# A retention loop with the output norm's channel gain moved into the output weight, and its loads in another order

## The chip, the cores and the metric

The kernel runs on one core of a Trainium2 chip. A core has a matrix engine (TensorE, PE in the profile; its weight loads are listed apart as PEld), a vector engine (DVE), a scalar engine (ACT), a general engine (POOL) and a sync engine (SP), which here issues most of the DMAs. Each engine works through its own queue in order; engines wait for one another by semaphores. The metric is the time of one execution on the device in microseconds.

## The reference

One inference step of a small decoder trunk with two layers: a retention layer and a sliding-window attention layer (called swa in the code), for a prompt of 1024 positions with 1024 channels and for 8 single new tokens, all in fp32. What bears on the change is the retention layer of the prompt:

```python
def retention_layer(x, S0, g_norm, w_in, g_out, w_out):
    h = rmsnorm(x, g_norm)
    proj = h @ w_in
    q, k, v, gate = jnp.split(proj, [RET_QK, 2 * RET_QK, 2 * RET_QK + RET_V], axis=-1)
    ...                       # 4 heads, 256 wide in q and k, 512 wide in v
    o, S = retention_scan(q, k, v, S0)      # 8 chunks of 128 positions
    o = rmsnorm(o, g_out.reshape(RET_HEADS, RET_DV)).reshape(B, L, RET_V)
    o = o * jax.nn.silu(gate)
    return x + o @ w_out, S.astype(S0.dtype)
```

`rmsnorm(o, g_out)` divides each row of a head's 512 channels by its root mean square and multiplies each channel by its gain. The gate is multiplied in after that, and then the 2048 channels are contracted with `w_out`. A gain per channel of `o` is therefore also a gain per row of `w_out`. The scan returns the final state of each head, 256 x 512, which is an output of its own.

## The kernel before, in words

fp32 matmuls are done as three passes over split operands: a number is held as `hi` (rounded) and `lo` (the rest), and hi x hi, hi x lo and lo x hi are added up. So each operand of a matmul needs two cheap steps on other engines: hi on ACT or DVE, lo on DVE or POOL.

The program goes through four stages. (1) The input projection, up to 546 us, writes q and k, v and the gate of every head and chunk to DRAM (`qks`, `vsc`, `gsc`). (2) The retention, up to about 708 us. (3) The output projection `ro_part`, up to about 905 us. (4) The attention layer.

The retention has 32 steps: heads (0,1) and then heads (2,3), and in each pair 8 chunks with the two heads in turn. A step has for its head and chunk:

- `b_qk`: PE forms the scores and transposes k (tile `tr`); DVE masks the scores (`sT`, L880), ACT and POOL split them (`sTh` L885, `sTl` L890); ACT and DVE make `kh` (L870) and `kl` (L875), ACT and POOL `vh` (L895) and `vl` (L900), DVE and POOL `qh` (L906) and `ql` (L912). In chunk 0 there is no state yet, and so neither `qh` nor `ql`.
- `b_mm`: PE adds to the state `S` (L922 to L924) and to the output `po` (L926 to L935).
- `b_Sh`, `b_Sl`: ACT and DVE split the new state (`Sh` L944, `Sl` L956). After a head's last chunk the scaled state goes to a tile `sf` (L948) instead, of tag `Sh` too, and is stored to DRAM by SP (L1068).
- `b_sq`, `b_ts`, `b_pw`: sum of squares of the output row (L963, tile `bss`), scale and epsilon (L967), power -1/2 on POOL (L118).
- `b_on` (L975): one DVE instruction multiplies `po` by that factor and by the channel gain `gbh`, a tile in which the head's 512 gains stand on all 128 partitions (loaded by `gbl`, L1002, once for each head).
- `b_tr`: PE transposes `on` (L103); `b_og` (L987): DVE multiplies it by the gate, tile `evw`; `b_oh` (L994) and `b_ol` (L998) split the product on ACT and POOL into the operand of the output projection (`A_hi`, `A_lo`, `B_hi`, `B_lo`).

ACT, DVE, POOL and SP run in the order in which the code issues their work. In each iteration `i` of the loop the function `others(i)` sets that order by hand: `og` of step i-2 comes first, then Sh, Sl, sq, ts, pw of step i-1, then the splits for step i+1, among them `on` of step i-1, and `sl` and `ql` of step i+1 come last. After `others` come the loads on SP's queue: `b_v(i+3)` (L754, `evx` or `evc`), `b_q(i+3)` (L746, `evp`) and `b_g(i)` (L760, `evw`). They are 256 KB each. The tiles come from rings of buffers: 3 for `evp` (tag p), 2 each for `evx`, `evc` and `evw` (tags x, c, w). A load waits on SP until the last reader of its ring buffer has finished, and everything behind it in SP's queue waits with it.

The first 128 output channels of the first half of positions are multiplied within the retention's last steps (`e_load`, `e_split`, `e_mm`; L1014, L1019, L1020, L1026 to L1028). The rest of the output projection takes its weights in slots of 1024 rows by 256 columns from `wslot`: two raw loads (`wr`, L1093), hi (`wh`) as a CAST on DVE (L1100) and lo (`wl`) as a subtraction on POOL (L1101), each over 128 x 1024. Its matmuls are L1160 to L1162.

Of the kernel before, what the change touches and what calls it, by code (L numbers as in the profile page):

```python
# [7 lines left out]
F32 = mybir.dt.float32  # L8
F32R = mybir.dt.float32r
AF = mybir.ActivationFunctionType  # L10
ALU = mybir.AluOpType
# [5 lines left out]
ND = 8  # L17
# [3 lines left out]
DV = 512  # L21
# [52 lines left out]
def _trunk(ctx, tc, nc, a):  # L74
    x_prompt, x_sample, state_ret = a["x_prompt"], a["x_sample"], a["state_ret"]
    cache_k, cache_v = a["cache_k"], a["cache_v"]
    norm_ret, ret_out_norm, norm_swa = a["norm_ret"], a["ret_out_norm"], a["norm_swa"]
    w_in_ret, w_out_ret = a["w_in_ret"][0], a["w_out_ret"][0]
    w_in_swa, w_out_swa = a["w_in_swa"][0], a["w_out_swa"][0]
    q_norm, k_norm, sinks = a["q_norm"], a["k_norm"], a["sinks"]  # L80
    y_p, y_s, nrp, nrs = a["y_p"], a["y_s"], a["nrp"], a["nrs"]
# [31 lines left out]
    gcol = cp.tile([128, 25], F32, name="gcol")  # L113
    gdec = cp.tile([128, 16, ND], F32, name="gdec")
# [12 lines left out]
    se = ExitStack()  # L127
    se.enter_context(tc.manual_schedule(engines={ET.Activation, ET.DVE, ET.Pool, ET.SP}))
    evp = se.enter_context(tc.tile_pool(name="evp", bufs=1, reuse_waits="tile"))
    M01 = evp.tile([128, 292], F32, name="M01")  # L130
    sa = ExitStack()
    dcp = sa.enter_context(tc.tile_pool(name="dcp", bufs=1, reuse_waits="tile"))
    wq = sa.enter_context(tc.tile_pool(name="wq", bufs=1, reuse_waits="tile"))
# [30 lines left out]

    def ring(tag):
        return evp.tile([128, 516], F32, tag="ev" + tag, bufs=EV[tag], name="ev" + tag)

    ADD, SUB, MUL = ALU.add, ALU.subtract, ALU.mult
    act, dve, pool = nc.scalar.activation, nc.vector, nc.gpsimd
# [73 lines left out]
    heads = [dict() for _ in range(H)]  # L243
# [166 lines left out]
    gb = sp.tile([128, D], F32, name="gb")  # L410
# [220 lines left out]
    n = 0  # L631
# [29 lines left out]
    raws = [(14.0,)] * 2 + [(20.0,)] * 2 + [(slots[14].t,)]  # L661
    raws = [x[0] for x in raws]
    raw_t = [0.0]
    for s in sets[2:]:
# [6 lines left out]
        v = s.kind == "v"  # L671
# [24 lines left out]
        for r in range(2 * s.subs):  # L696
            free = raws[-5] + 1.6
            need = min(reads[r])
            t = max(free, need - 13.0)
            t = raw_t[0] = max(t, raw_t[0] + 0.01)  # L700
# [4 lines left out]
        if v:  # L705
            n = len(slots)
# [17 lines left out]
    for h in range(H):  # L724
        t0 = max(t0 + GAP, sets[3 * h + 2].end + 10.0)
        for hf in range(2):
            for b in range(ND):
                d = {}
# [13 lines left out]
    def b_q(i):  # L742
        if i < len(steps):
            h, c = steps[i]
            t = ring("p")[:, 0:512].rearrange("p (j t) -> p j t", j=4)
            nc.sync.dma_start(out=t, in_=qks[h, c].rearrange("p (j t) -> p j t", j=4))  # L746
            heads[h].setdefault(("l", c), [None, None])[0] = t

    def b_v(i):
        if i < len(steps):  # L750
            h, c = steps[i]
            t = ring("xc"[i % 2])[:, 0:512]
            heads[h].setdefault(("l", c), [None, None])[1] = t
            nc.sync.dma_start(out=t, in_=vsc[h, c])  # L754

    def b_g(i):
        if i < len(steps):
            h, c = steps[i]
            t = heads[h]["g", c] = ring("w")[:, 0:512].rearrange("p (j t) -> p j t", j=4)
            nc.sync.dma_start(out=t, in_=gsc[h, c].rearrange("p (j t) -> p j t", j=4))  # L760

    def b_first():
        nc.sync.dma_start(out=M01[:, 0:256], in_=a["c1"][:, 128:384])
        nc.sync.dma_start(out=M01[:, 256:292], in_=a["c1"][:, 640:676])
        for i in range(2):
            b_q(i)
            b_v(i)
# [53 lines left out]
    for n in sorted(at):  # L821
        for fn, args in at[n]:
            fn(*args)
    rest = sorted([(t, 0, fn, args) for t, _, fn, args in ev] + [(t, 1, fn, args) for t, fn, args in pes],
                  key=lambda e: e[:2])
# [3 lines left out]
    sa.close()  # L829
    trp = ctx.enter_context(tc.tile_pool(name="trp", bufs=2, space=PSUM))  # L830

    wp0 = se.enter_context(tc.tile_pool(name="wp0", bufs=1, reuse_waits="tile"))
    sb = ExitStack()
    rp = sb.enter_context(tc.tile_pool(name="rp", bufs=1, reuse_waits="tile"))
    ap = ctx.enter_context(tc.tile_pool(name="ap", bufs=1, side="right", reuse_waits="tile"))
    A_hi = ap.tile([128, 8, NT], F32R, name="A_hi")
    A_lo = ap.tile([128, 8, NT], F32R, name="A_lo")
# [14 lines left out]
    M23 = rp.tile([128, 256], F32, name="M23")  # L852
    maskT = [M01[:, 0:128], M01[:, 128:256], M23[:, 0:128], M23[:, 128:256]]
    kdec = M01[:, 256:288].rearrange("p (h c) -> p h c", h=H)
    epsg = M01[:, 288:292]

# [82 lines left out]
    def b_Sh(h, c):  # L939
        d = heads[h]  # L940
        if c < NCH - 1:
            d["Sb"] = [rp.tile([128, 2, DV], F32R, name=nm, bufs=2) for nm in ("Sh", "Sl")]
            for f in range(2):
                act(d["Sb"][0][:, f], d["S"][f], AF.Copy, scale=GAM[h] ** (128.0 * (c + 1) - SREF))  # L944
        else:
            sf = rp.tile([128, 2, DV], F32, tag="Sh", bufs=2, name="sf")
            for f in range(2):
                act(sf[:, f], d["S"][f], AF.Copy, scale=GAM[h] ** SREF)  # L948
            sfs.append((h, sf))
# [22 lines left out]

    def b_on(h, c):
        d = heads[h]
        dve.scalar_tensor_tensor(d["on", c], d.pop(("po", c)), d["ss", c], d["gb"], MUL, MUL)  # L975

    def b_tr(h, c):
        d = heads[h]
# [18 lines left out]
        _, ol, ohf = o_at(h, c)  # L997
        pool.tensor_tensor(ol, heads[h].pop(("og", c)), ohf, SUB)  # L998

    def gbl(h):  # L1000
        t = rp.tile([128, DV], F32, name="gbh", bufs=2)
        nc.sync.dma_start(out=t, in_=ret_out_norm[0, h * DV:h * DV + DV].partition_broadcast(128))  # L1002
        heads[h]["gb"] = t

    ro_ps = {}
    e_hi = wp0.tile([128, 8, 128], F32R, name="eh")
    e_lo = wp0.tile([128, 8, 128], F32R, name="el")
    e_raw = []  # L1010

    def e_load(j):
        t = ring("p")[:, 0:512].rearrange("p (k f) -> p k f", k=4)
        nc.sync.dma_start(out=t, in_=w_out_ret[512 * j:512 * j + 512, 0:128].rearrange("(k p) f -> p k f", p=128))  # L1014
        e_raw.append(t)

    def e_split(j):
        js = slice(4 * j, 4 * j + 4)
        act(e_hi[:, js, :], e_raw[j], AF.Copy)  # L1019
        dve.tensor_tensor(e_lo[:, js, :], e_raw[j], e_hi.bitcast(F32)[:, js, :], SUB)  # L1020

    def e_mm():
        ps = ro_ps[0, 0] = trp.tile([128, 512], F32, name="tr")
# [7 lines left out]
    def at_step(fn, i):  # L1031
        if 0 <= i < len(steps):
            fn(*steps[i])

    def others(i):
        for fn, n in ((b_og, i - 2), (b_Sh, i - 1), (b_Sl, i - 1), (b_sq, i - 1), (b_ts, i - 1), (b_pw, i - 1),
                      (b_sT, i + 1), (b_qh, i + 1), (b_vh, i + 1), (b_on, i - 1), (b_oh, i - 2), (b_kh, i + 1),
                      (b_kl, i + 1), (b_sh, i + 1), (b_vl, i + 1), (b_ol, i - 2), (b_sl, i + 1), (b_ql, i + 1)):
            at_step(fn, n)

    b_q(2)
    b_g(0)
    b_v(2)
    gbl(0)
    b_g(1)
    gbl(1)
    nc.sync.dma_start(out=M23, in_=a["c1"][:, 384:640])
    for i in range(-1, len(steps) + 2):
        at_step(b_qk, i + 1)
        if i >= 0:  # L1050
            at_step(b_mm, i)
        others(i)
        if i in (31, 32):
            e_split(i - 31)
        if i == 32:
            e_mm()
        at_step(b_tr, i - 1)
        if i in (29, 30):
            e_load(i - 29)
        if i >= 0:  # L1060
            b_v(i + 3)
            b_q(i + 3)
            if i >= 2:
                b_g(i)
        if i in (15, 16):
            gbl(i - 13)
        for h, sf in sfs:
            nc.sync.dma_start(out=nrp[0, 0, h].rearrange("(f p) e -> p f e", p=128), in_=sf)  # L1068
        sfs.clear()

        if i == 15:
            dve.tensor_tensor(gdec, gdec, odT, MUL)
            dve.tensor_tensor(gdec, gdec, gcol[:, 0:16].unsqueeze(2).broadcast_to([128, 16, ND]), MUL)
        if i == 16:
            dve.tensor_copy(B_hi[:, :, 512:520], gdec)
            dve.tensor_tensor(B_lo[:, :, 512:520], gdec, B_hif[:, :, 512:520], SUB)
# [5 lines left out]
    wp = ctx.enter_context(tc.tile_pool(name="wp", bufs=1, reuse_waits="tile"))  # L1082
    hi_act = [False]
    lo_eng = [nc.gpsimd]

    def wslot(src):

        hi = wp.tile([128, 8, 256], F32R, tag="wh", bufs=3, name="wh")
        lo = wp.tile([128, 8, 256], F32R, tag="wl", bufs=3, name="wl")
        v = src.rearrange("(k p) f -> p k f", p=128)  # L1090
        for j in range(2):
            raw = wp.tile([128, 4, 256], F32, tag="wr", bufs=2, name="wr")
            nc.sync.dma_start(out=raw, in_=v[:, 4 * j:4 * j + 4, :])  # L1093
            step = 2 if hi_act[0] else 4
            for i in range(0, 4, step):
                js = slice(4 * j + i, 4 * j + i + step)
                if hi_act[0]:
                    nc.scalar.activation(hi[:, js, :], raw[:, i:i + step, :], AF.Copy)
                else:
                    nc.vector.tensor_copy(hi[:, js, :], raw[:, i:i + step, :])  # L1100
                lo_eng[0].tensor_tensor(lo[:, js, :], raw[:, i:i + step, :], hi.bitcast(F32)[:, js, :], ALU.subtract)  # L1101
        return hi, lo
# [26 lines left out]
    ro_slots = {}  # L1129
# [5 lines left out]
    def ro_ahead(n):  # L1135

        for key in ro_seq[len(ro_slots):n]:
            _, fp_, kh = key
            ro_slots[key] = wslot(w_out_ret[kh * 1024:kh * 1024 + 1024, fp_ * 256:fp_ * 256 + 256])

    O_hi, O_lo, _ = o_view(0)

# [634 lines left out]
    out = so_all()  # L1777
# [85 lines left out]
```

## Time and profile before

| | |
|---|---|
| median of 3 runs | 1357.28 us (1355.23 to 1359.15) |
| profiled execution | 1359.16 us, its span 1357.4 us |
| granted TensorE clock, mean | 0.989 |
| PE busy | 1313.8 us, 97% of the span |
| DVE, ACT, POOL busy | 744.6, 670.8, 759.8 us |
| HBM read, written | 129.11 MB, 57.41 MB |

The profile lists each instruction with its line, its engine, its start and length, and the idle time of the engine ahead of it with what released it. "PE tr L103 <- DVE on L975: 4.2, 2, 3.7" says that PE stood ahead of the transposes of line 103 until DVE's `on` was ready, 4.2 us in two places, 3.7 at the longest. SPq rows are the issues of DMAs on SP's queue: their start is when SP issued the load, not when the data landed. A window's row gives its length and then the busy time of each engine with the number of instructions, the granted clock, the mean busy share of the 16 DMA engines and GB/s.

### The profile page before, as it was taken

To read this page: it belongs to the slowest core of one execution; us is meant where nothing else is said; L and a number is where in the kernel's file an instruction comes from. 1 tells how busy PE (TensorE), PEld (TensorE's weight loads), DVE (VectorE), ACT (ScalarE), POOL (GpSimd) and SP (SyncE) were. 2 spreads that over 40 slices of the span, in tenths; PEclk is the share of its full clock that TensorE was granted. 3 is DMA by queue.
4 is the path that set the end of the run, shared out by engine and by line. 5 is a ranking of instruction groups with operands and counts; after the bars stand their busy time and mean duration, and the time that the engine had idled before them with its cause. 6 is when DMAs were issued, how large, how long until landed. Compare 5 with 4: busy or idle time off the path is not lost.

```text
span 1357.4 us, 25979 instructions
## 1 busy us (share of the span) xinstructions
PE 1313.8 (97%) x9541; PEld 1252.9 (92%) x9541; DVE 744.6 (55%) x1436; ACT 670.8 (49%) x1692; POOL 759.8 (56%) x886
## 2 busy tenths in 40 slices
PE   6999999999999999898989999999999999999998
PEld 6999999999999999787868889988999999998998
DVE  6943665656565653577762112334567777779321
ACT  5532555555565663576751111244576766667311
POOL 6753656656566663698976554563376666544000
PEclk9999999999999999999999999998999999999999
DMA  6314767677676762556546444451111111113533
GB/s 220 103 55 141 216 206 238 164 236 231 183 236 187 229 180 63 194 179 208 173 149 185 145 144 125 142 169 55 32 49 46 48 44 47 34 34 97 166 83 81
DMA packets 193859, 187.19 MB, mean 138 GB/s; under 512 B 12756, under 2 KB 173580, under 8 KB 193716
## 3 DMA queue, kind: packets, MB, share of 16 engines
q1 hardware_dynamic: 156832, 148.34, 35.8%
q10 hardware_dynamic: 36900, 37.19, 8.6%
q8 instruction: 75, 1.23, 0.4%
q14 instruction: 52, 0.43, 0.1%
HBM read 129.11 MB, written 57.41 MB: 137 GB/s over the span
## 4 chain that ended last, share of the span: by engine, by line
PE 84%; DVE 6%; POOL 3%; ACT 3%; DMA 2%; issue 2%; ACTq 0%; SPq 0%; POOLq 0%; DVEq 0%
PE b L340 7%; PE b L342 7%; PE b L341 7%; PE pj L1111 5%; PE pj L1112 5%; PE pj L1113 5%; PE pj L1160 4%; PE pj L1161 4%; PE pj L1162 4%; PE b L334 4%; PE b L333 4%; PE b L335 4%; PE tr L103 4%; PE S L922 1%; PE S L923 1%
## 5 line engine op out<-in xcount | busy, mean ns | idle before, releaser
L340 PE MATMUL b<-xh,woh 128*128 128x258 f32 x784 | 222.4, 284 | 0.0
L342 PE MATMUL b<-xh,wol 128*128 128x258 f32 x784 | 221.9, 283 | 0.0
L341 PE MATMUL b<-xl,woh 128*128 128x258 f32 x784 | 221.6, 283 | 0.0
L1111 PE MATMUL pj<-A_hi,wh 128*128 128x384 f32 (+1 forms) x512 | 173.0, 338 | 1.9 <-ACT Qd L1416 1.9
L1113 PE MATMUL pj<-A_hi,wl 128*128 128x384 f32 (+1 forms) x512 | 166.2, 325 | 0.0
L1112 PE MATMUL pj<-A_lo,wh 128*128 128x384 f32 (+1 forms) x512 | 166.2, 325 | 0.0
L1101 POOL TENSOR_TENSOR wl<-wr,wh 128x512 fp32r<-128x512 f32 (+1 forms) x68 | 124.6, 1844 | 50.5 <-DVE wh L1100 21.2
L340 PEld LDWEIGHTS b<-xh,woh 128*128 128x128 f32 x784 | 148.2, 189 | 1.2
L341 PEld LDWEIGHTS b<-xl,woh 128*128 128x128 f32 x784 | 148.8, 190 | 0.0
L342 PEld LDWEIGHTS b<-xh,wol 128*128 128x128 f32 x784 | 148.2, 189 | 0.0
L334 PE MATMUL b<-wol,xh 128*128 128x256 f32 x448 | 126.1, 282 | 1.2 <-DVE wol L224 1.2
L333 PE MATMUL b<-woh,xh 128*128 128x256 f32 x448 | 125.9, 281 | 0.0
L335 PE MATMUL b<-woh,xl 128*128 128x256 f32 x448 | 125.8, 281 | 0.0
L1527 POOL TENSOR_TENSOR s<-s,sm 128x512 f32<-128x512 f32 x64 | 67.6, 1058 | 76.5 <-DVE sm L1526 71.4
L282 POOL TENSOR_TENSOR yl<-yd,yh 128x256 fp32r<-128x256 f32 x64 | 56.3, 880 | 82.6 <-PE od L289 39.0
L1111 PEld LDWEIGHTS pj<-A_hi,wh 128*128 128x128 f32 x512 | 98.0, 191 | 2.4 <-ACT Qd L1416 2.2
L1112 PEld LDWEIGHTS pj<-A_lo,wh 128*128 128x128 f32 x512 | 98.0, 191 | 0.0
L1113 PEld LDWEIGHTS pj<-A_hi,wl 128*128 128x128 f32 x512 | 97.8, 191 | 0.0
L224 POOL TENSOR_TENSOR wol<-raw,woh 128x512 fp32r<-128x512 f32 x52 | 68.8, 1330 | 48.0 <-ACT woh L219 47.2
L334 PEld LDWEIGHTS b<-wol,xh 128*128 128x128 f32 x448 | 84.4, 188 | 1.4 <-DVE wol L224 1.4
L333 PEld LDWEIGHTS b<-woh,xh 128*128 128x128 f32 x448 | 84.4, 188 | 0.7
L335 PEld LDWEIGHTS b<-woh,xl 128*128 128x128 f32 x448 | 84.4, 188 | 0.0
(384 smaller groups left out, 3836.4 us busy)
## 6 DMA issues: line engine op xcount, KB each, us to landing
raw<-in_w_in_ret_dram ACTq DMA_DIRECT2D x44, 512.0 KB
st<-in_state_ret_dram SPq DMA_DIRECT2D x64, 256.0 KB
out_dram<-st SPq DMA_DIRECT2D x64, 256.0 KB
wr<-in_w_out_ret_dram SPq DMA_DIRECT2D x32, 512.0 KB
wr<-in_w_in_swa_dram SPq DMA_DIRECT2D x18, 512.0 KB
vb<-vscr SPq DMA_DIRECT2D x64, 128.0 KB
evp<-qks SPq DMA_DIRECT2D x32, 256.0 KB
evw<-gsc SPq DMA_DIRECT2D x32, 256.0 KB
```

What stands on the lines that cost most here:

```text
L224: eng.tensor_tensor(lo, src_of(s, name, sub), hi.bitcast(F32), SUB)
L333: mm(dst, xh, wh, start=a and i == 0, stop=False, skip_group_check=True)
L334: mm(dst, xh, wl, start=False, stop=False, skip_group_check=True)
L335: mm(dst, xl, wh, start=False, stop=z, skip_group_check=True)
L340: mm(dst, wh, xh, start=a, stop=False, **sg)
L341: mm(dst, wh, xl, start=False, stop=False, **sg)
L342: mm(dst, wl, xh, start=False, stop=z, **sg)
L1101: lo_eng[0].tensor_tensor(lo[:, js, :], raw[:, i:i + step, :], hi.bitcast(F32)[:, js, :], ALU.subtract)
L1111: mm(ps, hi[:, k, fs], xh[:, k, t0:t1], start=first and k == ks[0], stop=False)
L1112: mm(ps, hi[:, k, fs], xl[:, k, t0:t1], start=False, stop=False)
L1113: mm(ps, lo[:, k, fs], xh[:, k, t0:t1], start=False, stop=last and k == ks[-1])
L1527: nc.gpsimd.tensor_tensor(st[:, :, 0:256], st[:, :, 0:256], sm.unsqueeze(2).broadcast_to([128, 2, 256]), ALU.mult)
```

## The change

It does four things.

1. The gain `gbh` is gone: its four loads are not made, and `b_on` multiplies by the row factor alone. The same gains, as one number per partition (`gcol`), are put on the rows of the output weight. The slots of the output projection come from a new function `gslot`, which makes hi in eight ACT steps of 128 x 256 with the gain as scale, and lo in eight DVE steps `raw * gain - hi`. `e_split` does the same in four steps of 128 x 128 on each engine, one iteration earlier, and `e_load` loads three iterations earlier into a tile of its own (`er`). The multiplication of the new tokens' decay tile `gdec` by the gain is dropped.
2. The loads on SP: ahead of the loop q, v and g of the next steps come in another order, without `gbh`. In the loop `b_q(i + 4)`, `b_v(i + 4)`, `b_g(i)` are issued from i = -1 on.
3. The final state of an odd head takes a buffer of tag `Sl`, and the states that finish in iteration 30 or later are stored from ACT's queue.
4. Tiles are allocated in another order (`M01`, the pool `wp0`, a first unused tile in each ring and in the weight pool), so that they come to lie on other addresses. The number of buffers of the rings stays 3, 2, 2, 2.

```diff
     def b_on(h, c):
         d = heads[h]
-        dve.scalar_tensor_tensor(d["on", c], d.pop(("po", c)), d["ss", c], d["gb"], MUL, MUL)
+        dve.tensor_scalar(d["on", c], d.pop(("po", c)), d["ss", c], None, MUL)
...
-            sf = rp.tile([128, 2, DV], F32, tag="Sh", bufs=2, name="sf")
+            sf = rp.tile([128, 2, DV], F32, tag=("Sh", "Sl")[h % 2], bufs=2, name="sf")
...
     def e_load(j):
-        t = ring("p")[:, 0:512].rearrange("p (k f) -> p k f", k=4)
+        t = rp.tile([128, 4, 128], F32, name="er", bufs=2)
...
     def e_split(j):
-        js = slice(4 * j, 4 * j + 4)
-        act(e_hi[:, js, :], e_raw[j], AF.Copy)
-        dve.tensor_tensor(e_lo[:, js, :], e_raw[j], e_hi.bitcast(F32)[:, js, :], SUB)
+        for i in range(4):
+            k = 4 * j + i
+            gk = gcol[:, k:k + 1]
+            act(e_hi[:, k, :], e_raw[j][:, i, :], AF.Copy, scale=gk)
+            dve.scalar_tensor_tensor(e_lo[:, k, :], e_raw[j][:, i, :], gk, e_hi.bitcast(F32)[:, k, :], MUL, SUB)
...
     b_q(2)
+    b_v(2)
     b_g(0)
-    b_v(2)
-    gbl(0)
+    nc.sync.dma_start(out=M23, in_=a["c1"][:, 384:640])
     b_g(1)
-    gbl(1)
-    nc.sync.dma_start(out=M23, in_=a["c1"][:, 384:640])
     for i in range(-1, len(steps) + 2):
...
-        if i in (31, 32):
-            e_split(i - 31)
+        if i in (30, 31):
+            e_split(i - 30)
...
-        if i in (29, 30):
-            e_load(i - 29)
-        if i >= 0:
-            b_v(i + 3)
-            b_q(i + 3)
-            if i >= 2:
-                b_g(i)
-        if i in (15, 16):
-            gbl(i - 13)
+        b_q(i + 4)
+        b_v(i + 4)
+        if i >= 2:
+            b_g(i)
+        if i in (26, 27):
+            e_load(i - 26)
         for h, sf in sfs:
-            nc.sync.dma_start(out=nrp[0, 0, h].rearrange("(f p) e -> p f e", p=128), in_=sf)
+            eng = nc.scalar if i >= 30 else nc.sync
+            eng.dma_start(out=nrp[0, 0, h].rearrange("(f p) e -> p f e", p=128), in_=sf)
...
+    def gslot(kh, fp_):
+        raws = []
+        v = w_out_ret[kh * 1024:kh * 1024 + 1024, fp_ * 256:fp_ * 256 + 256].rearrange("(k p) f -> p k f", p=128)
+        for j in range(2):
+            raws.append(wraw())
+            nc.sync.dma_start(out=raws[j], in_=v[:, 4 * j:4 * j + 4, :])
+        hi, lo = wpair()
+        for k in range(8):
+            gk = gcol[:, 8 * kh + k:8 * kh + k + 1]
+            raw = raws[k // 4][:, k % 4, :]
+            nc.scalar.activation(hi[:, k, :], raw, AF.Copy, scale=gk)
+            nc.vector.scalar_tensor_tensor(lo[:, k, :], raw, gk, hi.bitcast(F32)[:, k, :], ALU.mult, ALU.subtract)
+        return hi, lo
```

SP's queue at the entry to the retention, before: the loads of q (`evp`), v (`evx`, `evc`), gate (`evw`), gain (`gbh`) and a mask.

```order
L746 DMA evp<-qks 128x512
L760 DMA evw<-gsc 128x512
L754 DMA evx<-vsc 128x512
L1002 DMA gbh<-in_ret_out_norm_dram 128x512
L760 DMA evw<-gsc 128x512
L1002 DMA gbh<-in_ret_out_norm_dram 128x512
L1047 DMA M_7721<-const_c_dram 128x256
L754 DMA evc<-vsc 128x512
L746 DMA evp<-qks 128x512
```

The same place in the changed kernel:

```order
L749 DMA evp<-qks 128x512
L757 DMA evx<-vsc 128x512
L763 DMA evw<-gsc 128x512
L1045 DMA M_7725<-const_c_dram 128x256
L763 DMA evw<-gsc 128x512
L749 DMA evp<-qks 128x512
L757 DMA evc<-vsc 128x512
L749 DMA evp<-qks 128x512
L757 DMA evx<-vsc 128x512
```

The two gains are gone, and the next q's follow closer behind.

SP's queue in the middle of the loop, two steps, before:

```order
L754 DMA evx<-vsc 128x512
L746 DMA evp<-qks 128x512
L760 DMA evw<-gsc 128x512
L754 DMA evc<-vsc 128x512
L746 DMA evp<-qks 128x512
L760 DMA evw<-gsc 128x512
```

The changed kernel there:

```order
L749 DMA evp<-qks 128x512
L757 DMA evx<-vsc 128x512
L763 DMA evw<-gsc 128x512
L749 DMA evp<-qks 128x512
L757 DMA evc<-vsc 128x512
L763 DMA evw<-gsc 128x512
```

q and v have changed places, and each is for one step later than before; the gate's load is for the same step as before.

DVE from the last steps of the retention into the output projection, before:

```order
L987 TENSOR_TENSOR og<-tr,evw 128x512
L967 TENSOR_SCALAR bss<-bss,M_84 128x1
L975 SCALAR_TENSOR_TENSOR on<-po,bss,gbh 128x512
L1020 TENSOR_TENSOR el<-evp,eh 128x512
L987 TENSOR_TENSOR og<-tr,evw 128x512
L1100 CAST wh<-wr 128x1024 x22
```

The changed kernel there:

```order
L990 TENSOR_TENSOR og<-tr,evw 128x512
L970 TENSOR_SCALAR bss<-bss,M_123 128x1
L978 TENSOR_SCALAR on<-po,bss 128x512
L990 TENSOR_TENSOR og<-tr,evw 128x512
L1107 SCALAR_TENSOR_TENSOR wl<-wr,gcol,wh 128x256 x88
```

The last piece of `el` now lies ahead of the second-last `og`, and behind the last `og` stand the short lo steps of the weight where the CASTs stood; hi has moved to ACT.

More of the change, by code (lines that the diff above doesn't have):

```diff
@@ L129, in _trunk @@
     evp = se.enter_context(tc.tile_pool(name="evp", bufs=1, reuse_waits="tile"))
-    M01 = evp.tile([128, 292], F32, name="M01")
     sa = ExitStack()
@@ L166, in ring @@
         return evp.tile([128, 516], F32, tag="ev" + tag, bufs=EV[tag], name="ev" + tag)
+    for tag in "wpxc":
+        ring(tag)
+    M01 = evp.tile([128, 292], F32, name="M01")
     ADD, SUB, MUL = ALU.add, ALU.subtract, ALU.mult
@@ L830, in _trunk @@
     trp = ctx.enter_context(tc.tile_pool(name="trp", bufs=2, space=PSUM))
-    wp0 = se.enter_context(tc.tile_pool(name="wp0", bufs=1, reuse_waits="tile"))
     sb = ExitStack()
     rp = sb.enter_context(tc.tile_pool(name="rp", bufs=1, reuse_waits="tile"))
+    wp0 = sb.enter_context(tc.tile_pool(name="wp0", bufs=1, reuse_waits="tile"))
     ap = ctx.enter_context(tc.tile_pool(name="ap", bufs=1, side="right", reuse_waits="tile"))
@@ L998, in b_ol @@
         pool.tensor_tensor(ol, heads[h].pop(("og", c)), ohf, SUB)
[L1000 to L1003, printed above, removed]
     ro_ps = {}
@@ L1072, in _trunk @@
             dve.tensor_tensor(gdec, gdec, odT, MUL)
-            dve.tensor_tensor(gdec, gdec, gcol[:, 0:16].unsqueeze(2).broadcast_to([128, 16, ND]), MUL)
         if i == 16:
@@ L1084, in _trunk, with wpair, wraw @@
     lo_eng = [nc.gpsimd]
+    nslot = [0]
+    def wpair():
+        n = nslot[0] % 3
+        nslot[0] += 1
+        return [wp.tile([128, 8, 256], F32R, tag=f"{nm}{n}", bufs=1, name=nm) for nm in ("wh", "wl")]
+    def wraw():
+        return wp.tile([128, 4, 256], F32, tag="wr", bufs=2, name="wr")
+    wp.tile([128, 8, 256], F32R, tag="wh2", bufs=1, name="wh")
+    def gslot(kh, fp_):
[11 more added lines that the diff above has]
+        return hi, lo
     def wslot(src):
-        hi = wp.tile([128, 8, 256], F32R, tag="wh", bufs=3, name="wh")
-        lo = wp.tile([128, 8, 256], F32R, tag="wl", bufs=3, name="wl")
+        hi, lo = wpair()
         v = src.rearrange("(k p) f -> p k f", p=128)
@@ L1138, in ro_ahead @@
             _, fp_, kh = key
-            ro_slots[key] = wslot(w_out_ret[kh * 1024:kh * 1024 + 1024, fp_ * 256:fp_ * 256 + 256])
+            ro_slots[key] = gslot(kh, fp_)
     O_hi, O_lo, _ = o_view(0)
```

## The prediction

> **What bounds the kernel now.** I read the page first, then the work of each engine by stage, then the waits of PE around the stages that the change touches, and last the instructions of one step. On the page PE is the full engine:
>
> ```profile
> PE 1313.8 (97%) x9541; PEld 1252.9 (92%) x9541; DVE 744.6 (55%) x1436; ACT 670.8 (49%) x1692; POOL 759.8 (56%) x886
> ```
>
> Only time in which PE stands, or runs at half pace, can be won; anything that makes PE stand is lost. By stage (length, then busy PE, PEld, DVE, ACT, POOL, granted clock, DMA share and GB/s):
>
> ```profile
> 640.00:695.00 55.00, 55.00 (x302) 46.63 (x301) 42.02 (x95) 40.20 (x96) 50.66 (x60) 1.00 0.48 155
> 715.00:810.00 95.00, 95.00 (x463) 78.92 (x462) 17.98 (x21) 11.71 (x35) 59.22 (x34) 0.99 0.51 157
> ```
>
> In the steady retention PE never stands, but POOL is busy for 92% and DVE for 76%: a step has little slack off PE. In the output projection the others have much room. PE's waits in the three windows 540-562, 612-640 and 695-720 us (total, times, longest):
>
> ```profile
> PE tr L103 <- DVE on L975: 1.8, 1, 1.8
> PE tr L863 <- DMA evp<-qks: 1.8, 1, 1.8
> ...
> PE tr L103 <- DVE on L975: 4.2, 2, 3.7
> ...
> PE tr L1162 <- POOL wl L1101: 3.3, 1, 3.3
> PE tr L1160 <- DVE wh L1100: 1.5, 1, 1.5
> PE tr L1028 <- DVE el L1020: 0.7, 1, 0.7
> ```
>
> So there are three holes: at the start, in the middle and at the end of the retention. The change works on each.
>
> **Start: no broadcast load of the norm weight, q before g.** DVE rows (start, length, in brackets the idle time before and its releaser):
>
> ```profile
> 555.10 0.75 DVE L975 SCALAR_TENSOR_TENSOR on<-po,bss,gbh 128x512 f32<-128x512 f32 x1 [2.32 <-DMA gbh<-in_ret_out_norm_dram]
> 556.67 0.69 DVE L987 TENSOR_TENSOR og<-tr,evw 128x512 f32<-128x512 f32 x1 [0.42 <-PE tr L103]
> ...
> 564.88 0.69 DVE L987 TENSOR_TENSOR og<-tr,evw 128x512 f32<-128x512 f32 x1 [3.13 <-PE tr L103]
> ```
>
> The first `on` waited 2.32 us for `gbh`; that wait goes. The rsqrt on POOL, some 0.6 us, is late next, so I take 2.0. The second `og` came 8.21 us after the first where the steady distance is 4.58 (below): 3.6 more, of which 1.8 is the wait for q and the rest half pace after it. The new order asks for q two loads earlier and puts no 256 KB broadcasts between: I take 3.5 of 3.6. Sum: -5.5 us (ends 0 and -5.9).
>
> **Middle: the final states.** A finished state `sf` takes a buffer of `Sh`, and the next head's `Sh` waits until its store has read it:
>
> ```profile
> 623.39 0.43 SPq L1068 DMA_DIRECT2D out_dram<-sf  x1
> 630.89 1.09 ACT L944 ACTIVATE Sh<-S 128x512 fp32r<-128x512 f32 x2 [3.61 <-DMA out_dram<-sf]
> 627.54 0.63 PE L103 MATMUL tr<-ident,on 128*128 128x128 f32 x4 [0.45 <-DVE on L975]
> 634.67 1.09 PE L103 MATMUL tr<-ident,on 128*128 128x128 f32 x4 [3.75 <-DVE on L975]
> ```
>
> With `sf` of the odd head in `Sl` the first head's `Sh` finds a free buffer; the second head's `Sh` and `Sl` still each meet a store of some 7.5 us, issued about 4.5 and 9 us earlier, so up to 1.4 us stays. PE wins at most 4.2 us of waits and about 1.3 of half pace (1.09 against 0.63 for four transposes). The vector engines cannot run these steps much faster than 4.2 us each, so of 5.5 about 3 can be had, and 1.8 if the step is already late for the reason below. I take -1.8 (ends 0 and -5.5). The dropped gdec multiply on DVE lies behind the same holes: 0.
>
> **End: the output weight scaled by row.** The split of the weight is cut in eight pieces, hi on ACT and lo on DVE, in place of CAST on DVE and 1024-wide subtractions on POOL:
>
> ```profile
> 707.20 0.69 DVE L987 TENSOR_TENSOR og<-tr,evw 128x512 f32<-128x512 f32 x1 [3.11 <-PE tr L103]
> 710.31 4.66 POOL L1101 TENSOR_TENSOR wl<-wr,wh 128x1024 fp32r<-128x1024 f32 x2
> 712.69 0.79 PE L1162 MATMUL tr<-A_hi,wl 128*128 128x512 f32 x1 [3.28 <-POOL wl L1101]
> ...
> 715.85 0.47 PE L1160 MATMUL tr<-A_hi,wh 128*128 128x512 f32 x1
> ...
> 717.09 0.39 PE L1162 MATMUL tr<-A_hi,wl 128*128 128x512 f32 x1
> ```
>
> From 712.69 PE needs 3.16 us for seven matmuls, afterwards 1.24 for five: about 1.4 us of half pace. The new first piece is ready after the last `og` (0.69) and `oh` (0.6), some 0.45 for hi and 0.48 for lo (a 128x256 step of DVE below). PE then starts within 2 us of its last transpose and never waits for a whole 1024-wide lo. The hole of 3.3 goes, the half pace of 1.4, and the 0.7 for `el`; about 1 us of new waits for hi and lo comes back. I take -4.2 (ends 0 and -5.4). Later slots: 8 x 0.48 = 3.8 us of ACT and of DVE for each of 16 slots, in a stage where both are idle for over 80%: hidden, 0. POOL loses its lo work there, which also hides.
>
> **The loop: where the gate's load now stands.** In the code before a step issues v, q, g: `b_q(i+3)` waits until `ql(i)` has read its buffer, and `b_g(i)` stands behind it. Now a step issues `b_q(i+4)`, `b_v(i+4)`, `b_g(i)`, and ring p still has three buffers. So `b_q(i+4)` waits for `ql(i+1)`, a step later, and SP's queue holds `b_g(i)`, which feeds `og(i)` two steps on, behind it. One step in the trace of before, DVE and POOL:
>
> ```profile
> 592.36 0.69 DVE L987 TENSOR_TENSOR og<-tr,evw 128x512 f32<-128x512 f32 x1 [0.58 <-PE tr L103]
> 592.97 1.28 DVE L956 SCALAR_TENSOR_TENSOR Sl<-S,Sh 128x512 fp32r<-128x512 f32 x2
> 594.17 0.20 DVE L967 TENSOR_SCALAR bss<-bss,M 128x1 f32<-128x1 f32 x1
> ...
> 595.88 0.47 DVE L875 SCALAR_TENSOR_TENSOR kl<-tr,M,kh 128x256 fp32r<-128x256 f32 x1
> 596.95 0.69 DVE L987 TENSOR_TENSOR og<-tr,evw 128x512 f32<-128x512 f32 x1 [0.59 <-PE tr L103]
> ...
> 601.53 0.69 DVE L987 TENSOR_TENSOR og<-tr,evw 128x512 f32<-128x512 f32 x1 [0.59 <-PE tr L103]
> ...
> 594.51 0.66 POOL L118 TENSOR_TENSOR bss<-bss,mhalf 128x1 f32<-128x1 f32 x1 [0.28 <-DVE bss L967]
> 595.15 1.30 POOL L900 TENSOR_TENSOR vl<-evx,vh 128x512 fp32r<-128x512 f32 x1
> 596.40 1.28 POOL L998 TENSOR_TENSOR A_lo<-og,A_hi 128x512 fp32r<-128x512 f32 x1
> 597.64 0.46 POOL L890 TENSOR_TENSOR sTl<-sT,sTh 128x128 fp32r<-128x128 f32 x1
> 598.06 0.74 POOL L912 TENSOR_TENSOR ql<-evp,qh 128x256 fp32r<-128x256 f32 x1
> ```
>
> From an `og` at 592.36 the work runs without a gap through Sl, the two `bss`, vl, the lo of `og`, sTl and ql, which ends at 598.80: 6.44 us. SP's issues, and shares of the DMA in stretches of other steps:
>
> ```profile
> 589.68 0.32 SPq L746 DMA_DIRECT2D evp<-qks  x1
> 594.26 0.32 SPq L746 DMA_DIRECT2D evp<-qks  x1
> 594.68 0.37 SPq L760 DMA_DIRECT2D evw<-gsc  x1
> ...
> 656.87 0.32 SPq L746 DMA_DIRECT2D evp<-qks  x1
> ...
> 592.80:593.30 0.50, 0.50 (x5) 0.42 (x4) 0.50 (x2) 0.50 (x2) 0.50 (x2) 1.00 0.60 225
> 598.00:598.30 0.30, 0.30 (x3) 0.26 (x2) 0.30 (x2) 0.30 (x3) 0.30 (x2) 1.00 0.02 7
> 661.30:661.80 0.50, 0.50 (x4) 0.41 (x3) 0.50 (x4) 0.50 (x2) 0.20 (x2) 1.00 0.05 16
> ```
>
> Today g for the `og` at 601.53 is issued at 594.68, 6.85 us ahead, and nobody waits. In the new order it is the third load of a burst that begins when ql ends at 598.80. A burst of three is over 3.4 us after its q was issued (589.68 to about 593.1), 3.8 (594.26 to 598.0) or 4.8 (656.87 to 661.7); I take 4.0 with the semaphore. So `og(i)` cannot start earlier than 6.44 + 0.03 + 4.0 + 0.05 = 10.5 us after `og(i-2)`, where it is 601.53 - 592.36 = 9.17 today: 1.36 per two steps, 0.68 per step. PE works 4.58 us a step and cannot cover it; it will stand before the transposes that wait for `on`. The steps that lead into chunk 0 of the second pair have no ql and those after the last q are free, which leaves 24 bound steps, and one that the lead of the start absorbs: 23 x 0.68 = +15.7 (ends +9 with 3.4 us, 23 x 0.39, and +25 with 4.8 us, 23 x 1.09).
>
> **The sum.** -5.5 - 1.8 - 4.2 + 15.7 = +4.2 us. The profiled run took 1359.16 us for a span of 1357.4, 1.9 above the median 1357.28 of the three runs; against that median I expect 1361.5. A measurement of this kernel tells about 0.3%, 4.1 us, from no change (so 1353.2 to 1361.4), and the forecast lies at that edge.
>
> A clock rule speaks further against the change. The rows show the clock full after a gap of 0.45 us (627.54) and half after one of 3.75 (634.67); gaps of 0.7 in each step are not in the trace. The Trainium skill, "TensorE: Matmul & The Clock Gate", section "A second HAM failure mode: psum-queue depth-cycling", says that frequent short idle times between groups of matmuls can make the clock swing between half and full. By the row the gaps cost only themselves; what half pace would do is the third rival.
>
> **The rivals.**
> - The g load is in time after all (a buffer of ring p free earlier, or slack that lets ql run earlier): then only the holes go, -5.5 - 3 - 4.2, 1344.6 us. For it: the three holes are real and in the chain. Against: the 6.44 us are dense work of two in-order engines. It decides from a landing below 2.7 us (9.17 - 6.44). This one ends on the faster side. Chance 0.19.
> - The chain holds, and landing is near its long end, since q, v and g now all start behind one ql: +25 - 11.5, some 1371 us. Against: the bursts of before have the same size. Chance 0.09.
> - Half pace in each bound step: one swing cost about 1.4 us at 712.69; on half of 23 steps that is +16 on top, 1377. Chance 0.06. The skill's page named above would have it so; the clock of 1.00 in the steady stretch speaks neither way, since it has no gaps.
> - The row-wise split keeps PE waiting in the first slots, since ACT and DVE take 3.8 us each where PE wants the first pieces at once: the end gives nothing, 1365.7. Chance 0.08.
>
> **How the numbers follow.** The likeliest, the chain at 3.8 to 4.2 us, has 0.58; its own range is 1356 to 1367. It lies on both sides of the edge: slower 0.24, within 0.28, faster 0.06. The first rival gives faster 0.16, within 0.03; the others slower 0.21, within 0.02. Together faster 0.22, within 0.33, slower 0.45. The range from 1346 to 1371 leaves out the best of the first rival and the half pace.
>
> **What would show it.** Right: PE's waits `tr <- DVE on` (or on Sl) of some 15 us in all between 560 and 700, with `og` on DVE idle before it until DMA `evw`, steps of 5.26 us, evp issued at the end of a ql and evw 0.9 us behind; no wait for `gbh`; the wait for `wl` gone at the end. Wrong: `og` released by PE in the steady part, steps of 4.58, or a stretch of the retention with a clock well under 0.95. A surprise could come from the entry to the attention stage at 905-920, whose POOL and DVE queues get other work ahead; I cost it at 0 because PE's wait there hangs on work that the change does not touch, and any shift would show as another wait of PE in that window.

## The result, and the profile after

The changed kernel is slower: 1369.47 us in the median of 4 runs (1367.80 to 1372.61), against 1357.74 for the kernel before beside it. The ratio is 1.0095, with a 95% interval of 1.0079 to 1.0111; the medians lie 11.7 us apart. The time lies in the range given, near its upper end; the likeliest value, 1361.5, is 8 us short.

The profiled execution took 1367.80 us, its span 1366.0. On its page TensorE is busy for 4 us less than before, in a span 8.6 longer:

```profile
PE 1309.6 (96%) x9541; PEld 1245.9 (91%) x9541; DVE 768.9 (56%) x1537; ACT 728.2 (53%) x1826; POOL 681.4 (50%) x854
```

By stage (length, busy PE, PEld, DVE, ACT, POOL, clock, DMA share, GB/s) the retention has lost its full use of PE, while the output projection is still full:

```profile
540.00:556.00 16.00, 15.15 (x103) 13.28 (x102) 7.93 (x19) 9.78 (x25) 7.51 (x14) 1.00 0.84 262
556.00:615.00 59.00, 51.26 (x277) 42.17 (x276) 38.33 (x88) 37.61 (x88) 46.13 (x55) 1.00 0.44 143
...
640.00:705.00 65.00, 56.88 (x306) 46.34 (x306) 43.15 (x98) 42.02 (x98) 52.15 (x62) 1.00 0.46 150
...
725.00:820.00 95.00, 95.00 (x456) 78.59 (x455) 35.14 (x85) 44.73 (x115) 10.16 (x14) 0.99 0.55 168
```

Where before no wait of PE stood between 640 and 695, the waits of PE in the windows 565-630, 630-650 and 650-705 now read (total, times, longest), 20.4 us in all where the forecast had some 15:

```profile
PE tr L103 <- DVE on L978: 9.2, 7, 2.0
...
PE tr L103 <- DVE on L978: 3.4, 2, 3.0
...
PE tr L103 <- DVE on L978: 7.8, 7, 1.4
```

and behind them stand the waits of DVE from 560 to 712:

```profile
DVE og L990 <- DMA evw<-gsc: 34.0, 18, 4.0
DVE on L978 <- POOL bss L118: 12.8, 28, 0.8
DVE og L990 <- PE tr L103: 5.7, 9, 1.1
```

The gate's load releases 18 of the 32 `og`; before it released none. One turn of the chain, in rows of DVE, POOL, SP and DVE again (start, length, idle time before and releaser):

```profile
565.52 0.69 DVE L990 TENSOR_TENSOR og<-tr,evw 128x512 f32<-128x512 f32 x1 [2.23 <-DMA evw<-gsc]
566.13 1.28 DVE L959 SCALAR_TENSOR_TENSOR Sl<-S,Sh 128x512 fp32r<-128x512 f32 x2
567.33 0.20 DVE L970 TENSOR_SCALAR bss<-bss,M 128x1 f32<-128x1 f32 x1
...
567.67 0.66 POOL L118 TENSOR_TENSOR bss<-bss,mhalf 128x1 f32<-128x1 f32 x1 [1.94 <-DVE bss L970]
568.31 1.26 POOL L903 TENSOR_TENSOR vl<-evc,vh 128x512 fp32r<-128x512 f32 x1
569.53 1.27 POOL L1001 TENSOR_TENSOR A_lo<-og,A_hi 128x512 fp32r<-128x512 f32 x1
...
571.18 0.75 POOL L915 TENSOR_TENSOR ql<-evp,qh 128x256 fp32r<-128x256 f32 x1
...
571.96 0.32 SPq L749 DMA_DIRECT2D evp<-qks  x1
572.38 0.38 SPq L757 DMA_DIRECT2D evx<-vsc  x1
572.85 0.38 SPq L763 DMA_DIRECT2D evw<-gsc  x1
...
576.91 0.69 DVE L990 TENSOR_TENSOR og<-tr,evw 128x512 f32<-128x512 f32 x1 [2.93 <-DMA evw<-gsc]
```

SP issues q 0.03 us after `ql` has ended, and the `og` that needs the third load starts 4.95 us later. The starts of the `og` in the two profiles (us), counted from 0, so that number 1 is the second, show where time came and went:

```
og      before   after    difference
 1      564.88   559.31     -5.57     start
13      619.83   625.41     +5.58     12 steps: +11.15
17      641.26   647.33     +6.07     middle: +0.49
27      687.01   700.75    +13.74     10 steps: +7.67
first full-pace matmul of the output projection
        715.85   727.12    +11.27     end: -2.47
```

### The profile page after: what moved, and what is told of

Same layout as the page of the kernel before. It is cut to its first block, busy times and chain, and to the rows that moved or that the text cites. A ratio compares the mean times of both kernels' runs of the same rounds, so it can differ in the third digit from the quotient of the medians.

```text
span 1366.0 us, 26150 instructions
## 1 busy us (share of the span) xinstructions
PE 1309.6 (96%) x9541; PEld 1245.9 (91%) x9541; DVE 768.9 (56%) x1537; ACT 728.2 (53%) x1826; POOL 681.4 (50%) x854
## 4 chain that ended last, share of the span: by engine, by line
PE 76%; DVE 9%; POOL 5%; DMA 4%; ACT 2%; issue 2%; SPq 1%; ACTq 0%; POOLq 0%; DVEq 0%
PE b L343 7%; PE b L345 7%; PE b L344 7%; PE pj L1134 5%; PE pj L1135 5%; PE pj L1136 5%; PE pj L1183 4%; PE pj L1184 4%; PE pj L1185 4%; PE b L337 4%; PE b L336 4%; PE b L338 4%; DMA evw<-gsc 4%; PE tr L103 3%; DVE Sl L959 1%
## 5 line engine op out<-in xcount | busy, mean ns | idle before, releaser
L1217 POOL TENSOR_TENSOR acc<-acc,sq 128x256 f32<-128x256 f32 (+1 forms) x28 | 20.6, 742 | 146.8 <-ACT sq L1216 146.7
L1107 DVE SCALAR_TENSOR_TENSOR wl<-wr,gcol,wh 128x256 fp32r<-128x256 f32 x128 | 54.0, 488 | 70.3 <-ACT wh L1106 67.9
```

## The experiments

Theory A is that of the prediction: the gate's load is held in SP's queue behind a q load that waits one step longer. All ratios are to the kernel before on the same chip. The runs were not all made on one chip, so two runs are compared by their ratios or by the rows of their profiles; the difference of two medians is only rough.

**The gate first.** In the changed kernel the gate's load goes ahead of q and v:

```diff
-        b_q(i + 4)
-        b_v(i + 4)
         if i >= 2:
             b_g(i)
+        b_q(i + 4)
+        b_v(i + 4)
```

> The changed kernel, with the gate's load moved ahead of the loads of q and v within each step, all else as changed. Theory A (the gate's load is held in SP's queue behind a q load that waits one step longer, and each og waits for it): the wait for evw on DVE and nearly all PE waits of 560 to 700 us go; only the gains at the start (5.5), middle (about 3) and end (5.1, from the profiles: 13.7 at the last og, 8.6 at the end of the span) stay, so 1357.7 - 13.6 = about 1344, between 1342 and 1348. Theory B (other addresses of the tiles, or the other edits of the change, slow the loop): it stays near 1369. Theory C (the three loads landing together contend): about half of the difference returns, 1357.

Measured: 1345.30 us, ratio 0.9930 (0.9906 to 0.9954). DVE from 560 to 684 waits for no gate any more:

```profile
DVE og L990 <- PE tr L103: 17.4, 26, 2.0
DVE on L978 <- POOL bss L118: 12.2, 27, 0.7
DVE bss L970 <- ACT on L966: 0.6, 1, 0.6
```

This one edit is worth 24.2 us by the medians and some 22 us by the ratios. It leaves theory B, other addresses or other edits as the cause, nothing to explain; theory C, the three loads in each other's way, would have left 1357. The kernel with the gate first is faster than both kernels.

**The gate second.** Order q, gate, v:

```diff
         b_q(i + 4)
-        b_v(i + 4)
         if i >= 2:
             b_g(i)
+        b_v(i + 4)
```

> The changed kernel with the order q, gate, v in each step: the gate still stands behind the q load that waits, but lands second and not third. Theory A: in the bursts of the changed kernel the second load is over some 3.0 us after the q issue and the third 4.0, so the distance of two ogs shrinks from 10.9 by 1.0 to about 9.9, against 9.16 unbound: 0.35 us a step remain, 8 us over 23 steps, so about 1344 + 8 = 1352 (1349 to 1357). Theory B: 1369. Theory C (contention of the burst, whatever its order): 1366 to 1369.

Measured: 1355.41 us, ratio 0.9986 (0.9971 to 1.0001), within the 1349 to 1357 of theory A. DVE's wait for the gate from 560 to 700:

```profile
DVE og L990 <- DMA evw<-gsc: 20.5, 18, 1.9
```

In its profile `og` 2 stands at 564.48 and `og` 14 at 624.34: 9.98 us for two steps, where 9.9 was worked out. The wait shrinks with the place in the burst; that is a dose, not a switch.

**The loop's loads alone.** The kernel before with the changed kernel's loop loads, their order and the step for which they load:

```diff
-        if i >= 0:
-            b_v(i + 3)
-            b_q(i + 3)
-            if i >= 2:
-                b_g(i)
+        b_q(i + 4)
+        b_v(i + 4)
+        if i >= 2:
+            b_g(i)
```

> The kernel before, with the changed kernel's loop order alone (q, v of step i+4, gate of step i, from i = -1); broadcast gain, weight split, final states and addresses as before. Theory A: 24 bound steps at 0.86 us are 20 us, of which the holes at start and middle, which stay, hide some 5: about 1373 (1369 to 1379), with og waiting for evw. Theory B: no change, 1356 to 1359.

Measured: 1376.86 us, ratio 1.0153 (1.0113 to 1.0193). On DVE from 560 to 700:

```profile
DVE og L987 <- DMA evw<-gsc: 31.9, 18, 2.7
```

So the loop's new loads cost 19 to 21 us by themselves (medians, ratio); none of the other edits is needed for it. Whether the order does it or the step, the run with one number put back tells.

**The old loop in the changed kernel**, the reverse of the last edit:

> The changed kernel with the loop loads of before put back (v, q of step i+3, gate of step i, from i = 0), all else as changed. Theory A: as with the gate first, about 1344 to 1348; what lies above it is what the earlier start of the q loads is worth. Theory B: 1369.

Measured: 1348.83 us, ratio 0.9943 (0.9924 to 0.9963). Its second `og` starts at 561.28, 1.4 us later than with the gate first, and PE waits 1.5 us for a q load at the start: that is what q four steps ahead is worth.

**One number.** The changed kernel's order q, v, gate, with q for step i+3:

```diff
-        b_q(i + 4)
+        if i >= 0:
+            b_q(i + 3)
         b_v(i + 4)
```

> The changed kernel with one number put back: q is loaded for step i+3 and not i+4 (from i = 0); order q, v, gate, v for step i+4, all else as changed. Theory A (the step for which q is loaded sets which ql SP waits for; the order alone does not hurt): q waits for the ql of the step before, as in the kernel before, the gate is issued in time although it still stands third, nobody waits for evw: 1344 to 1349. Rival (the gate third in a burst is late by itself): the gate lands 4.4 us after the q issue in the same step, which would show as waits for evw and 1352 or more.

Measured: 1347.36 us, ratio 0.9927 (0.9901 to 0.9954), and no `og` waits for the gate. Third place does no harm when the q in front of it does not wait for this step's `ql`: it is the step for which q is loaded, together with the place behind q, that costs the time, and not the order by itself.

**Another queue.** The gate's load issued by ACT, at its place in the code:

```diff
-            nc.sync.dma_start(out=t, in_=gsc[h, c].rearrange("p (j t) -> p j t", j=4))
+            nc.scalar.dma_start(out=t, in_=gsc[h, c].rearrange("p (j t) -> p j t", j=4))
```

> The changed kernel with its own order of the loads, but the gate's load issued from ACT's queue instead of SP's; q and v stay on SP. Theory A (what costs is that the gate stands in SP's queue behind the waiting q load): the gate is issued when ACT comes to it, some 2 us after the og that frees its buffer, nobody waits for evw, about 1345 as with the gate first, plus up to 4 if ACT's issue of 0.4 us a step counts: 1343 to 1350. Theory D (it is the work asked for at one time, or where the gate stands in the code, not the queue): 1366 to 1370.

Measured: 1347.53 us, ratio 0.9931 (0.9915 to 0.9947); no wait for the gate either. The same loads in the same order of the code cost nothing that this run shows once they do not share the queue.

The next runs take the gains apart.

**No gain in the kernel before.** `gbl` and the multiplication by `gbh` taken out:

> The kernel before without the gain of the output norm: its four broadcast loads and the multiplication by them are left out, everything else as before. Theory A for the start (the broadcasts hold up on, and the q loads behind them): the first og 2.0 us and the second 4 to 5.5 us earlier, 1357.7 - 5 = about 1353 (1351 to 1355). Rival (the late q alone makes the hole, by its place in the queue): the second og at most 2.5 us earlier, 1355 to 1357.

Measured: 1350.71 us, ratio 0.9951 (0.9936 to 0.9966), faster than either side expected. The first two `og` come 1.8 and 4.1 us earlier, as theory A had it. But the middle changed too: `og` 17 stands at 634.03, 7.2 us earlier than before, and so 3.1 us more than at the second `og`. ACT from 610 to 650, first in the kernel before and then in this one:

```profile
ACT Sh L944 <- PE po L935: 5.8, 4, 2.1
ACT Sh L944 <- DMA out_dram<-sf: 4.3, 2, 3.6
...
ACT Sh L944 <- PE po L935: 6.1, 5, 1.2
ACT sf L948 <- PE po L935: 2.5, 2, 1.3
```

The wait for the stores of `sf` is gone although their buffers are as before. Two of the broadcasts had stood in SP's queue right there, at 623.00 and 627.43. That they had made the stores slow is a guess; the next run speaks against it as the only cause.

**The final states in `Sh` again**, in the kernel with the gate first:

```diff
-            sf = rp.tile([128, 2, DV], F32, tag=("Sh", "Sl")[h % 2], bufs=2, name="sf")
+            sf = rp.tile([128, 2, DV], F32, tag="Sh", bufs=2, name="sf")
```

> The changed kernel with the gate's load first (1345.3) and the final state of the odd heads in a buffer of tag Sh again, as before the change. Theory: the next pair's first Sh waits for a store once more, so the wait of PE before on grows from 2.0 us to some 5 and half pace follows: 2 to 4 us slower, 1347 to 1350, seen between the ogs 13 and 17 of the profile. Rival (the store is no longer late since the loop lost its broadcasts at that place): within 0.5 us.

Measured: 1348.85 us, ratio 0.9943 (0.9928 to 0.9958), 1.8 us above the kernel with the gate first by the ratios and 3.6 by the medians. The intervals overlap, so the profile has to tell: `og` 17 stands at 637.65 and not at 634.05, and on ACT from 610 to 650 the wait is back:

```profile
ACT Sh L947 <- DMA out_dram<-sf: 3.9, 1, 3.9
```

So with the new loads the tag does matter, while the run without the gain, with the old loads, the old tag and no broadcasts, has no such wait. No broadcast is left in this run either, and yet `Sh` starts 7.1 us after its store was issued (618.87 to 625.99), where it was 7.5 us before the change (623.39 to 630.89); in the run without the gain `Sh` started 4.7 us after the issue (618.51 to 623.22) and did not wait. What makes the store slow in the one and not in the other is not shown.

**The old split of the output weight**, in the kernel with the gate first. This kernel leaves the gain out of those columns:

```diff
-            ro_slots[key] = gslot(kh, fp_)
+            ro_slots[key] = wslot(w_out_ret[kh * 1024:kh * 1024 + 1024, fp_ * 256:fp_ * 256 + 256])
```

> The changed kernel with the gate's load first (1345.3) and the output weight split as before: hi 128x1024 on DVE, lo 128x1024 on POOL, the gain left off those columns (computes without it there). From the profiles (last og to the first full-pace matmul: 8.65 us before, 6.2 with the new split) 2.5 us slower, about 1348. Rival: 4.2 us, as the forecast had it, 1349.5; or none, if the output projection catches up.

Measured: 1350.52 us, ratio 0.9956 (0.9941 to 0.9971), 3.5 us above by the ratios and 5.2 by the medians, with intervals that overlap. PE from 690 to 725 has the old hole:

```profile
PE tr L1185 <- POOL wl L1124: 3.3, 1, 3.3
PE tr L1183 <- DVE wh L1123: 1.4, 1, 1.4
PE tr L103 <- DVE on L978: 1.1, 1, 1.1
```

From the last `og` to the first matmul at full pace it is 10.1 us here (699.55 to 709.63) and 6.6 us with the gate first (700.10 to 706.66). The profile gives the new split 3.5 us, between the 2.5 and the 4.2 that were expected.

**The early split spread over four steps**, on the kernel with the gate first:

```diff
-        for i in range(4):
-            k = 4 * j + i
+        for i in range(2 * (j % 2), 2 * (j % 2) + 2):
+            k = 4 * (j // 2) + i
...
-        if i in (30, 31):
-            e_split(i - 30)
+        if 28 <= i <= 31:
+            e_split(i - 28)
```

> The changed kernel with the gate's load first (1345.3), and the early split of the output weight's first columns in two pieces for each of the iterations 28 to 31 instead of four in 30 and 31. In the profile with the gate first PE stands 1.1 us before on where four pieces (1.3 us of DVE) lie ahead of og; with two (0.65 us, about DVE's idle time in a step) that goes: 1 us less in the profile between og 28 and og 31, 1344 to 1345, too little for the times to tell. Rival: two pieces in four steps delay each step by 0.1 to 0.6 us, and nothing is won.

Measured: 1348.08 us, ratio 0.9933 (0.9910 to 0.9956). PE's wait for `on` from 684 to 700 is 0.9 us in two places, against 1.1 in one; `og` 31 stands at 700.03 against 700.10. Nothing is won, as the rival had it. Two pieces took not 0.65 us but 1.63 to 1.65 in three of the four steps, and `og` 27, 28 and 29 come 5.46 us after the one before instead of 4.58: 0.9 us each, more than the rival's 0.1 to 0.6.

## Why the prediction came out as it did

**The loop** had the right mechanism and the right first half. The chain from an `og` to the end of the `ql` of its step was given as 6.44 us and SP's answer as 0.03; the rows above give 565.52 to 571.93 and 571.96. The second half was sized too small. It was "4.0 with the semaphore", from the end of the burst. The rows of the DMA in the turn shown are:

```profile
575.90:576.20 0.30, 0.30 (x3) 0.25 (x2) 0.00 (x0) 0.30 (x1) 0.30 (x1) 1.00 0.07 27
576.20:576.90 0.70, 0.70 (x5) 0.58 (x4) 0.00 (x0) 0.13 (x1) 0.21 (x1) 1.00 0.00 0
```

The burst was over by 576.2 at the latest, 4.2 us after the q issue, and `og` started at 576.91. Over the 18 `og` that the gate released, the time from q's issue to `og` is 4.50 us in the mean (3.97 to 5.86). In most of them about 0.4 us pass between the last data and the start, where I had put 0.05. So two steps are held to 6.44 + 0.03 + 4.5 = 10.97 us; `og` 2 to `og` 12 measure 620.27 - 565.52 = 54.75, or 10.95 for each two. The two bound stretches cost 11.15 + 7.67 = 18.8 us where the sum had 15.7: 3.1 us of the miss, and within the ends given, 9 and 25.

**The start** was right: -5.57 at the second `og`, -5.5 in the sum. The run without the gain shows that the broadcasts made most of it, 4.1 us at the second `og`.

**The middle** is the second step that failed: +0.5 and not -1.8, outside the ends of 0 and -5.5. The gain itself is real, 2.1 us between `og` 13 and `og` 17 with the gate first (614.71 to 634.05, against 619.83 to 641.26). But the chain of the gate reaches into it: `og` 14 waited 3.97 us for a gate issued 4.97 us before, while five more loads and a store of `sf` were issued behind it. That they slowed it down is likely from this row, but was not tried. PE then stood for 3.03 us and ran at half pace behind it:

```profile
635.01 1.08 PE L103 MATMUL tr<-ident,on 128*128 128x128 f32 x4 [3.03 <-DVE on L978]
```

The work from 635.01 to 638.45, 3.44 us, takes 1.83 us in the next step (640.34 to 642.17), and the granted clock from 632 to 640 was 0.79. So the half pace that the change was to remove there came back by another wait, about 1.6 us of it. And the reason given for the middle was only half of it: with the old loads the wait for the store also goes without the new tag, in the run that leaves out the gain.

**The end** is the third: -2.5 and not -4.2. The wait for the 1024-wide lo went, but not the half pace:

```profile
722.72 0.51 PE L1183 MATMUL tr<-A_hi,wh 128*128 128x512 f32 x1 [1.84 <-ACT wh L1106]
...
723.96 0.79 PE L1185 MATMUL tr<-A_hi,wl 128*128 128x512 f32 x1 [0.51 <-DVE wl L1107]
...
726.69 0.62 PE L1185 MATMUL tr<-A_hi,wl 128*128 128x512 f32 x1
727.12 0.42 PE L1183 MATMUL tr<-A_hi,wh 128*128 128x512 f32 x1
```

From 723.96 to 727.12 seven matmuls take the same 3.16 us as before. And the four pieces of the early split on DVE ahead of an `og` bring a wait of PE of some 1.1 us that was put at 0. They took 2.85 us, the four of the second split 1.47 (in rows of DVE, POOL and DVE again):

```profile
709.06 2.85 DVE L1021 SCALAR_TENSOR_TENSOR el<-er,gcol,eh 128x128 fp32r<-128x128 f32 x4
...
709.20 1.35 POOL L1001 TENSOR_TENSOR B_lo<-og,B_hi 128x512 fp32r<-128x512 f32 x1
710.51 0.51 POOL L893 TENSOR_TENSOR sTl<-sT,sTh 128x128 fp32r<-128x128 f32 x1
710.98 0.79 POOL L915 TENSOR_TENSOR ql<-evp,qh 128x256 fp32r<-128x256 f32 x1
...
714.03 1.47 DVE L1021 SCALAR_TENSOR_TENSOR el<-er,gcol,eh 128x128 fp32r<-128x128 f32 x4
```

A piece takes 0.34 us where POOL is idle; the two beside `B_lo` and `sTl` took 1.37 and 0.55 us. That POOL's work holds them up fits these rows, but was not tried. The later slots cost nothing, as forecast: PE is full from 725 to 820.

The terms add up: -5.57 + 11.15 + 0.49 + 7.67 - 2.47 = +11.27 at the first full-pace matmul, against +4.2. Of these 7.1 us the loop missed 3.1, the middle 2.3 and the end 1.7, all the same way. The range reached as far as 1371 for a longer landing; that it had room for the middle and the end as well was luck. The profiled spans differ by only 8.6, because what comes after, most of which the change does not touch, took 638.9 us in this execution and 641.55 in the other; the medians, 11.7 apart, agree with the 11.3.

**The rivals.** The gate was not in time, so the faster one fell; it shows its value in the runs where the gate is freed: medians of 1345 to 1349 where 1344.6 was worked out, and by the ratios 8 to 10 us less than before where it had 12.7. The landing near its long end, 1371, came closest in time, though not because the burst was long, but because what follows it is; the longer wait made only 3.1 of the 9.3 us that this rival adds. Half pace from short gaps did not come: PE stood 7.7 us of the 59 from 556 to 615, in pieces of up to 2.0, at a granted clock of 1.00. The swing that the Trainium skill, "TensorE: Matmul & The Clock Gate", section "A second HAM failure mode: psum-queue depth-cycling", describes for frequent short idle times is not seen in this stretch. Within the retention half pace came only in the middle, behind the gap of 3.03 us. The row-wise split did leave PE waiting in its first slot, by 1.84 + 0.51 us; it was still a gain.

## What to carry to other kernels

In a queue that works in order, a load prefetched one step deeper on the same ring of buffers is not earlier once the ring is full: it waits for a later release, and takes everything behind it along. Before moving loads within a step, write down for each what its issue waits for, and put the one that is needed soonest ahead of the one that waits longest, or on another queue. A price taken from where data end is short of the time until the reader starts: take it from a row in which something really waited for such a load.

## What the runs showed that was not expected

The same gap did not always bring half pace. In the kernel with the gate second PE stood for the same 1.84 and 0.50 us ahead of the output projection:

```profile
710.12 0.50 PE L1183 MATMUL tr<-A_hi,wh 128*128 128x512 f32 x1 [1.84 <-ACT wh L1106]
...
711.35 0.50 PE L1185 MATMUL tr<-A_hi,wl 128*128 128x512 f32 x1 [0.50 <-DVE wl L1107]
711.69 0.39 PE L1183 MATMUL tr<-A_hi,wh 128*128 128x512 f32 x1
```

and the next matmul was at full pace at once, with a granted clock of 1.00 from 700 to 720, where the changed kernel needed 3.16 us for seven. In the six other runs with the new split half pace came, with a clock of 0.91 in that window. A forecast can give such a place a chance, but no certain price.

In the attention stage, whose code is the same in all these kernels, executions differ by some 3 to 4 us: from the first transposes of `kd` (904.64 with the gate first, 912.11 with it second) to the end of the span (1348.4 and 1352.2) it is 443.8 and 440.1 us, at a granted clock of 0.98 and 0.99. That is about the spread of the runs of one kernel, and why the changes of 1 to 3 us were read from the profile's rows and not from the times.
